# Padding and types of narrow matmuls in two causal attentions: last key block, masks, first query block

## The chip, the cores and the metric

The kernel runs on one core of a Trainium2 chip. The metric is the device time of one launch in microseconds, the median over runs. The core has five engines with instruction streams of their own that wait for each other through semaphores: PE (TensorE, matmuls; its weight loads are listed apart as PEld), DVE (VectorE), ACT (ScalarE), POOL (GpSimd) and SP (here only an issuer of transfers).

## The reference

A hybrid decoder block on 1024 tokens of width 1024, with 16 learned meta tokens in front. Three groups of heads work side by side on the same normalised input: 8 heads of stick-breaking attention (width 64), a Mamba-2 state-space mixer, and 8 heads of MLA (multi-head latent attention). Their outputs go through one output projection, then comes a SwiGLU. What matters here are the two attentions, both causal, in blocks of 128 queries:

```python
# stick-breaking
mask = (kidx[None, :] < qidx[:, None]) & valid[None, :]
z = jnp.einsum('bqhd,bkhd->bhqk', qb, kf) * scale
log_1m = jnp.where(mask, jax.nn.log_sigmoid(-z), 0.0)
between = lax.cumsum(log_1m, axis=3, reverse=True) - log_1m
w = jnp.exp(jnp.where(mask, jax.nn.log_sigmoid(z) + between, -jnp.inf))
out = jnp.einsum('bhqk,bkhd->bqhd', w, vf)
...
# MLA
mask = (kidx[None, :] <= qidx[:, None]) & valid[None, :]
s = jnp.einsum('bqhd,bkhd->bhqk', qb, kf) * scale
p = jax.nn.softmax(jnp.where(mask, s, -1e30), axis=-1)
out = jnp.einsum('bhqk,bkhd->bqhd', p, vf)
```

## The kernel before

**Precision.** Most matmuls take 4-byte operands in the type `F32R` (fp32r, a reduced fp32 that PE takes in one instruction). To keep fp32 accuracy a value is split in two: `hi` is its copy in F32R (by ACT), `lo` is value minus `hi` (by DVE or POOL), and a product becomes three matmuls: hi by hi, lo by hi, hi by lo. The profile writes both F32 and F32R matmul operands as `f32`. Some smaller products, as those of the state-space mixer (lines 797, 801, 810) and the row spreading (line 181), are in plain F32.

**Stages, in the order of time.** The first projections (to about 82 us); stick-breaking attention in four pairs of heads (82 to 482 us), with projections of the next pair and the convolutions of the mixer (`conv_unit`, through `dense_fm`, lines 137 to 139) woven in; the mixer's chunks and the latent projections (to 687 us); MLA, head by head (687 to 1085 us), with the gates of the mixer (`gate_units`) and the first output rows (`out_rows`) woven in; the rest of the output projection and the SwiGLU (to the end).

**Who sets the order.** The program is written stage by stage; a planner with a timeline model puts the instructions of each engine in an order that mixes stages by priority and readiness. On each engine the instructions then run in that order.

**A row of scores.** Keys are counted with the 16 meta tokens first, so query block i (0 to 7) sees 16 + 128 (i + 1) keys. `key_chunks(i)` (line 46) cuts them into chunks of at most 512 columns. For block 0 there are 144 keys, and the chunk is `max(n, 256)` = 256 columns wide: the matmul computes 112 columns that nobody reads. `sb_row` (line 654) makes two F32R matmuls per chunk (lines 662, 663), `mla_row` (line 945) three (960 to 962). In the last chunk of a row the causal mask is added by one more matmul into the same PSUM bank: identity (weights) times a 128x128 mask of 0 and -1e30 (lines 666 and 965), both in bf16 (`identb`, `sb_mask`, `mla_mask`, made at lines 97 to 114). Then ACT or DVE reads the bank, only up to column `n_all - c0`.

**The weighted values.** `weighted_values` (line 293) takes two query blocks at a time, 2j (`pe_even`) and 2j + 1 (`pe_odd`), for j = 0 to 3. PE transposes the weights in groups g = 0 to j of two key blocks each (lines 325, 327), ACT and DVE split them into `ph` and `pl` (`split`, lines 306 to 312), and `accumulate` multiplies them with the values into the bank `out`. A key block has 256 columns: 128 for the odd query block, then 128 for the even one. In the last group (g = j) the second key block is seen by the odd query block only. Its other 128 columns, 384 to 511 of `ph` and `pl`, are set to zero by POOL (lines 330, 331) so that the product is 256 wide all the same, and its two matmuls (lines 300, 301) close the accumulation. There are 8 heads in each attention and 4 values of j, so 64 last groups in all.

**Other names that matter below.** `load_w` (line 119) loads and splits a weight tile through the buffer with the tag `wraw`, of which there is one. `spread` (line 176) and all transposes use `ident`, the 128x128 identity.

Of the kernel before, what the change touches and what calls it, by code (L numbers as in the profile page):

```python
# [11 lines left out]
F32 = mybir.dt.float32  # L12
F32R = mybir.dt.float32r
BF16 = mybir.dt.bfloat16
I32 = mybir.dt.int32
AF = mybir.ActivationFunctionType
ALU = mybir.AluOpType
# [20 lines left out]
NEG = -1e30  # L38
# [7 lines left out]
def key_chunks(i):  # L46
    n = 16 + 128 * (i + 1)
    if n <= 512:
        return [(0, max(n, 256))]
    blocks = i + 1  # L50
    if n <= 1024 and blocks <= 7:
        first = (blocks + 1) // 2 if blocks < 7 else 3
        a = 16 + 128 * first
        return [(0, a), (a, n - a)]
    a = 16 + 128 * 2
    return [(0, a), (a, 384), (a + 384, 384)]
# [3 lines left out]
def tile_hybrid_block(ctx: ExitStack, tc: tile.TileContext, a: dict):  # L60
    nc = tc.nc
    act, dve, pool, pe, sp = nc.scalar, nc.vector, nc.gpsimd, nc.tensor, nc.sync
# [6 lines left out]
    def f32(ap):  # L69
        return ap.bitcast(F32)  # L70
# [3 lines left out]
    const = ctx.enter_context(tc.tile_pool(name="const", bufs=1))  # L74
# [19 lines left out]
    s_inv = dram.tile([MLA_HEADS, SEQ], F32, name="s_inv")  # L94


    ident = const.tile([128, 128], F32, name="ident")
    make_identity(nc, ident)
    identb = const.tile([128, 128], BF16, name="identb")
    act.activation(identb, ident, AF.Identity)  # L100
    ones = const.tile([128, 128], F32, name="ones")
    dve.memset(ones, 1.0)
    zcol = const.tile([128, 1], F32, name="zcol")
    dve.memset(zcol, 0.0)
    halfcol = const.tile([128, 1], F32, name="halfcol")
    dve.memset(halfcol, 0.5)
    sb_mask = const.tile([128, 128], BF16, name="sb_mask")
    mla_mask = const.tile([128, 128], BF16, name="mla_mask")
    for m, base in ((sb_mask, -1), (mla_mask, 0)):
        pool.memset(m, 0.0)  # L110
        pool.affine_select(
            out=m, in_=m, pattern=[[-1, 128]], compare_op=ALU.is_ge, fill=NEG,
            base=base, channel_multiplier=1,
        )
    gmix = const.tile([128, KT], F32, name="gmix")
    sp.dma_start(gmix, a["gmix"])

# [175 lines left out]
    def weighted_values(tp, pvp, work, j, rows, V, hh, dram_out, pm, base=None):  # L293

        pe_even, pe_odd = rows
        out = pvp.tile([128, 512], F32, tag="pv", name="pv")

        def accumulate(blk, ph, pl, c, last):
            if last:
                pe.matmul(out[:64, :256], V[:, blk, hh, 0:64], pl[:, c : c + 256], start=False, stop=False)  # L300
                pe.matmul(out[:, :256], V[:, blk, hh, :], ph[:, c : c + 256], start=False, stop=True)
            else:
                pe.matmul(out[:, :256], V[:, blk, hh, :], ph[:, c : c + 256], start=False, stop=False)  # L303
                pe.matmul(out[:64, :256], V[:, blk, hh, 0:64], pl[:, c : c + 256], start=False, stop=False)

        def split(pt, n):
            nb = 4 if work is not sbb else 2
            ph = work.tile([128, 512], F32R, tag="ph", bufs=nb, name="ph")
            pl = work.tile([128, 512], F32R, tag="pl", bufs=nb, name="pl")
            act.copy(ph[:, :n], pt[:, :n])  # L310
            dve.tensor_tensor(pl[:, :n], pt[:, :n], f32(ph[:, :n]), op=ALU.subtract)  # L311
            return ph, pl

        pt = tp.tile([128, 512], F32, tag="tp", name="ptm")
        pe.transpose(pt[:META, 0:128], pe_odd[:, 0:META], ident)
        pe.transpose(pt[:META, 128:256], pe_even[:, 0:META], ident)
        act.copy(pm[:META], pt[:META, :256])
        dve.tensor_tensor(pm[32 : 32 + META], pt[:META, :256], f32(pm[:META]), op=ALU.subtract)
        pe.matmul(out[:, :256], V[:, 0, hh, :], pm, start=True, stop=False)
        for g in range(j + 1):  # L320
            last = g == j
            pt = tp.tile([128, 512], F32, tag="tp", name="ptg")
            for e in range(2):
                k0 = META + 128 * (2 * g + e)
                pe.transpose(pt[:, e * 256 : e * 256 + 128], pe_odd[:, k0 : k0 + 128], ident)  # L325
                if not (last and e == 1):
                    pe.transpose(pt[:, e * 256 + 128 : e * 256 + 256], pe_even[:, k0 : k0 + 128], ident)  # L327
            ph, pl = split(pt, 384 if last else 512)
            if last:
                pool.memset(f32(ph[:, 384:512]), 0.0)  # L330
                pool.memset(f32(pl[:, 384:512]), 0.0)
            accumulate(2 * g + 1, ph, pl, 0, False)
            accumulate(2 * g + 2, ph, pl, 256, last)
        half = work.tile([64, 256], F32, tag="half", bufs=1, name="half")
        if base is None:
            act.copy(half, out[64:128, :256])
        else:
            for e in range(2):
                c = slice(128 * e, 128 * (e + 1))
                i = 2 * j + 1 - e  # L340
                act.activation(half[:, c], out[64:128, c], AF.Identity, bias=base[64:128, hh, i : i + 1])
        oT = work.tile([64, 256], F32, tag="oT", bufs=2, name="oT")
        dve.tensor_tensor(
            oT.rearrange("p (b t) -> p b t", b=2)[:, ::-1, :],
            out[:64, :256].rearrange("p (b t) -> p b t", b=2),
            half.rearrange("p (b t) -> p b t", b=2),
            op=ALU.add,
        )
        act.dma_start(dram_out[:, 256 * j : 256 * (j + 1)], oT)
# [286 lines left out]
    for i, (q0, qn) in enumerate(((0, 256), (256, 384), (640, 384))):  # L636
# [3 lines left out]
        c0, n = CH_ALL[i]  # L640
# [8 lines left out]
    with ctx_sb as st:  # L649
        sbb = st.enter_context(tc.tile_pool(name="sbb", bufs=2, side="right", reuse_waits="tile"))  # L650
        sc = st.enter_context(tc.tile_pool(name="sc1", bufs=3, space=PSUM, reuse_waits="tile"))
        pvp = st.enter_context(tc.tile_pool(name="pv1", bufs=1, space=PSUM, reuse_waits="tile"))

        def sb_row(Qh, Kh, KSh, i):
            n_all = META + 128 * (i + 1)
            cm = sbb.tile([128, T], F32, tag="cm", bufs=4, name="cm")
            qs = Qh[:, 128 * i : 128 * (i + 1)]
            chunks = key_chunks(i)
            for c0, n in chunks[::-1]:
                ps = sc.tile([128, 512], F32, tag="sc", name="sc_ps")  # L660
                last = c0 + n >= n_all
                pe.matmul(ps[:, :n], qs, Kh[:, c0 : c0 + n], start=True, stop=False)
                pe.matmul(ps[:, :n], qs, KSh[:, c0 : c0 + n], start=False, stop=not last)
                if last:
                    m0 = n_all - 128 - c0
                    pe.matmul(ps[:, m0 : m0 + 128], identb, sb_mask, start=False, stop=True)
                    n = n_all - c0
                act.activation(cm[:, c0 : c0 + n], ps[:, :n], AF.Sigmoid, scale=-0.125)  # L668
            rev = cm[:, 0:n_all][:, ::-1]
            dve.tensor_tensor_scan(rev, rev, zcol.to_broadcast([128, n_all]), 1.0, ALU.mult, ALU.add)  # L670
            return cm

        pms = meta_tiles(sbb)

        def sb_attend(p, proj, values):
            Q, K, KS = proj
            for h in range(2):
                for j in range(NQ // 2):  # L680
                    rows = [sb_row(Q[h], K[h], KS[h], 2 * j + e) for e in range(2)]
                    weighted_values(tp, pvp, sbb, j, rows, values[0], h, s_osb[p, 64 * h : 64 * (h + 1)], pms[j % 2], values[1])

        values = load_value_steps(sbv, sbb, 0)
        step_sizes()
        convs = [8, 9, 10, 11, 0, 1, 2, 3, 4, 5, 6, 7]
        for p in range(4):
            sb_attend(p, proj, values)
            if p < 3:
                if p == 1:  # L690
                    sb_values(1, [load_w(a["w_sbv"][1, u]) for u in range(2)], range(9))
                proj, k_evac, q_evac = sb_project(p + 1)
                dense_fm(dpool, load_w(a["w_sbk"][p + 1]), KT, 128, hn_mov, CH_ALL, k_evac)
                dense_fm(dpool, load_w(a["w_sbq"][p + 1]), KT, 128, hn_real, CH_REAL, q_evac)
                values = load_value_steps(sbv, sbb, p + 1)
            for u in convs[3 * p : 3 * p + 3]:
                conv_unit(u)
# [224 lines left out]
    with ExitStack() as st:  # L922
# [22 lines left out]
        def mla_row(proj, i, total):  # L945
# [11 lines left out]
            for x, (c0, n) in enumerate(chunks):  # L957
# [4 lines left out]
                pe.matmul(ps[:, :n], qh, KL[:96, c0 : c0 + n], start=False, stop=not last)  # L962
                if last:
                    m0 = n_all - 128 - c0
                    pe.matmul(ps[:, m0 : m0 + 128], identb, mla_mask, start=False, stop=True)
                    n = n_all - c0
                dve.tensor_reduce(sm[:, x : x + 1], ps[:, :n], AX.X, ALU.max, negate=True)
                banks.append((ps, c0, n))
# [24 lines left out]
        V = None  # L993
# [760 lines left out]
```

## Time and profile before

| | |
|---|---|
| median of 3 runs | 1889.12 us (1889.0 to 1889.23) |
| the profiled execution | 1887.26 us, of which its span 1885.5 |
| mean granted TensorE clock | 0.962 |

The profile covers one execution. Times are from the start of the span. A row of the page's list of groups, or of the list by line, reads: line, engine, operation, what is written and what is read, the shape of the weights and of the moving operand or output, type, count; then the busy time in us and the mean duration of one in ns; then the idle time of the engine just before these instructions, and what ended it. A row in order of time reads: start, length in us, engine, line, operation, operands, count. Busy time of PE is the union of durations that overlap each other, and their ends are modelled; so distances between starts tell more of what a matmul costs. In a table of stretches the columns are: the stretch, its length, then the busy time and the count for PE, PEld, DVE, ACT and POOL (with a filter only those engines that it leaves), the granted clock, the busy share of the DMA engines and the GB/s.

### The profile page before, as it was taken

Reading aid. Unit: us, or ns where it says so; the run is one execution under the profiler, and the core shown is the slowest. Engines: PE = TensorE matmul, PEld = TensorE weight load, DVE = VectorE, ACT = ScalarE, POOL = GpSimd, SP = SyncE. Lnnn points to the kernel's source line nnn. Section 1 sums busy time; section 2 is a strip of 40 time slices with the busy share of each in tenths; the row PEclk is TensorE's granted clock in tenths of the full one; section 3 lists DMA queues with packets and bytes.
Section 4 is the critical chain, followed back from the end, with each engine's and each line's share of the span. In section 5 each row is a group of like instructions: output and inputs, shape, how many; then the busy total and the mean of one; then the engine's idle time right before and its main releaser. Section 6 shows DMA issues by size and latency. Waiting matters only on the chain.

```text
span 1885.5 us, 26687 instructions
## 1 busy us (share of the span) xinstructions
PE 1730.0 (92%) x9724; PEld 1501.6 (80%) x9724; DVE 1322.4 (70%) x2025; ACT 866.0 (46%) x1881; POOL 880.6 (47%) x707
## 2 busy tenths in 40 slices
PE   8889999999999889996989778889999999799997
PEld 7879989999877679985878657678888888677787
DVE  8888567776546734455565699986667766899956
ACT  7555555555566546674444234432222223433333
POOL 3443244243565465553221266653344333688782
PEclk9999999999999989997999889999999999899998
DMA  4221132122634554454332513122222224733102
GB/s 151 56 73 64 57 80 74 52 60 72 167 105 139 180 164 106 107 130 150 57 72 91 129 50 112 49 86 79 82 88 83 76 75 136 280 100 109 47 0 90
DMA packets 124615, 182.75 MB, mean 97 GB/s; under 512 B 29490, under 2 KB 86804, under 8 KB 124484
## 3 DMA queue, kind: packets, MB, share of 16 engines
q1 hardware_dynamic: 105088, 165.49, 29.3%
q10 hardware_dynamic: 19396, 15.56, 2.7%
q8 instruction: 76, 1.25, 0.3%
q14 instruction: 55, 0.45, 0.1%
HBM read 129.51 MB, written 51.50 MB: 96 GB/s over the span
## 4 chain that ended last, share of the span: by engine, by line
PE 61%; DVE 15%; DMA 7%; issue 4%; POOL 3%; ACT 3%; SPq 1%; ACTq 0%; DVEq 0%; POOLq 0%
PE b_ps L1327 7%; PE b_ps L1329 7%; PE b_ps L1328 7%; PE d_ps L137 6%; PE d_ps L139 6%; PE d_ps L138 6%; DVE raw L1070 2%; DMA gy<-s_y 2%; PE b_ps L1528 2%; PE b_ps L1530 2%; PE b_ps L1529 2%; DVE op L1067 2%; PE ptg L325 1%; DMA raw<-s_ossm 1%; PE pv L303 1%
## 5 line engine op out<-in xcount | busy, mean ns | idle before, releaser
L137 PE MATMUL d_ps<-hnh,whi 128*128 128x384 f32 (+6 forms) x744 | 248.9, 335 | 7.8 <-DVE go L535 4.0
L139 PE MATMUL d_ps<-hnl,whi 128*128 128x384 f32 (+6 forms) x744 | 246.1, 331 | 0.0
L138 PE MATMUL d_ps<-hnh,wlo 128*128 128x384 f32 (+6 forms) x744 | 245.9, 331 | 0.0
L126 POOL TENSOR_TENSOR wlo<-wraw,whi 128x1024 fp32r<-128x1024 f32 (+1 forms) x51 | 124.7, 2445 | 180.9 <-ACT whi L124 171.8
L1067 POOL TENSOR_TENSOR op<-raw,op 128x512 fp32r<-128x512 f32 x113 | 174.3, 1573 | 57.2 <-ACT op L1066 54.0
L137 PEld LDWEIGHTS d_ps<-hnh,whi 128*128 128x128 f32 (+1 forms) x744 | 140.9, 189 | 12.9 <-DVE go L535 5.5
L311 DVE TENSOR_TENSOR pl<-ptg,ph 128x512 fp32r<-128x512 f32 (+1 forms) x160 | 99.5, 629 | 64.5 <-ACT ph L310 62.8
L138 PEld LDWEIGHTS d_ps<-hnh,wlo 128*128 128x128 f32 (+1 forms) x744 | 140.7, 189 | 2.3 <-issue 0.2
L139 PEld LDWEIGHTS d_ps<-hnl,whi 128*128 128x128 f32 (+1 forms) x744 | 140.6, 189 | 2.4 <-issue 0.2
L1327 PE MATMUL b_ps<-T,wh 128*128 128x512 f32 x352 | 138.4, 394 | 0.7 <-ACT T L1066 0.7
L1066 ACT CAST op<-raw 128x512 fp32r<-128x512 f32 x149 | 84.1, 618 | 117.2 <-PE d_ps L1530 46.9
L1328 PE MATMUL b_ps<-T,wl 128*128 128x512 f32 x352 | 137.1, 390 | 0.5 <-POOL wl L1067 0.5
L1329 PE MATMUL b_ps<-T,wh 128*128 128x512 f32 x352 | 137.6, 392 | 0.0
L1067 POOL TENSOR_TENSOR wlo<-raw,whi 128x1024 fp32r<-128x1024 f32 (+1 forms) x22 | 53.0, 2410 | 150.5 <-ACT whi L1066 150.5
L670 DVE TENSOR_TENSOR_SCAN cm<-cm,zcol 128x144 f32<-128x144 f32 (+3 forms) x64 | 101.2, 1586 | 13.0 <-ACT cm L668 12.2
L310 ACT CAST ph<-ptg 128x512 fp32r<-128x512 f32 (+1 forms) x160 | 85.6, 543 | 36.7 <-PE ptg L327 28.7
L1067 POOL TENSOR_TENSOR wl<-raw,wh 128x512 fp32r<-128x512 f32 x46 | 70.6, 1545 | 62.2 <-ACT wh L1066 62.2
L1070 DVE TENSOR_TENSOR raw<-raw 128x512 f32<-128x512 f32 x58 | 70.9, 1227 | 40.4 <-DMA raw<-in_w_gate_dram 35.8
L1066 ACT CAST wh<-raw 128x512 fp32r<-128x512 f32 x88 | 53.0, 616 | 73.7 <-PE b_ps L1329 66.0
L492 POOL TENSOR_TENSOR csig<-csig,cacc 128x384 f32<-128x384 f32 (+1 forms) x36 | 47.8, 1328 | 83.0 <-ACT csig L491 50.6
L487 DVE SCALAR_TENSOR_TENSOR cacc<-d_ps,cw,cacc 128x384 f32<-128x384 f32 (+3 forms) x108 | 61.8, 573 | 33.6 <-ACT cacc L480 31.5
L1528 PE MATMUL b_ps<-op 128*128 128x512 f32 x183 | 73.7, 408 | 12.6 <-DVE hF L1073 11.3
(447 smaller groups left out, 5434.3 us busy)
## 6 DMA issues: line engine op xcount, KB each, us to landing
raw<-in_w_gate_dram SPq DMA_DIRECT2D x22, 512.0 KB
raw<-in_w_up_dram SPq DMA_DIRECT2D x22, 512.0 KB
s_hid<-gs SPq DMA_DIRECT2D x44, 256.0 KB
raw<-in_w_down_dram SPq DMA_DIRECT2D x22, 512.0 KB
raw<-s_hid SPq DMA_DIRECT2D x22, 512.0 KB
wraw<-in_w_xbc_dram SPq DMA_DIRECT2D x12, 512.0 KB
wraw<-in_w_o_dram SPq DMA_DIRECT2D x10, 512.0 KB
s_xs<-csig SPq DMA_DIRECT2D x24, 192.0 KB
```

What stands on the lines that cost most here:

```text
L126: pool.tensor_tensor(lo[:, :cols], raw[:, :cols], f32(hi[:, :cols]), op=ALU.subtract)
L137: pe.matmul(ps[:m, :n], wh, mh, start=(kt == 0), stop=False)
L138: pe.matmul(ps[:m, :n], wl, mh, start=False, stop=False)
L139: pe.matmul(ps[:m, :n], wh, ml, start=False, stop=(kt == nkt - 1))
L670: dve.tensor_tensor_scan(rev, rev, zcol.to_broadcast([128, n_all]), 1.0, ALU.mult, ALU.add)
L1066: act.copy(hi, value)
L1067: eng.tensor_tensor(lo, value, f32(hi), op=ALU.subtract)
L1070: dve.tensor_tensor(out, x, y, op=ALU.subtract)
L1327: pe.matmul(banks[j], hi[:, ks], UH[u][k], start=start and k == 0, stop=False, skip_group_check=skip)
L1328: pe.matmul(banks[j], lo[:, ks], UH[u][k], start=False, stop=False, skip_group_check=skip)
L1329: pe.matmul(banks[j], hi[:, ks], UL[u][k], start=False, stop=stop and k == 3, skip_group_check=skip)
L1528: pe.matmul(banks[o], wh[:, os], hh, start=first, stop=False, skip_group_check=not start)
```

## The change

The last key block of a group is multiplied with its 128 own query columns only, and is taken before the block next to it, so that the full 256 columns are closed last; the memsets go. The masks and the identity that multiplies them become F32R, made in an F32 scratch tile and copied by ACT; `ident` becomes an F32 view of the F32R identity. `key_chunks(0)` is 144 columns wide instead of 256.

```diff
 def key_chunks(i):
     n = 16 + 128 * (i + 1)
     if n <= 512:
-        return [(0, max(n, 256))]
+        return [(0, n)]
...
-    ident = const.tile([128, 128], F32, name="ident")
-    make_identity(nc, ident)
-    identb = const.tile([128, 128], BF16, name="identb")
-    act.activation(identb, ident, AF.Identity)
+    scratch = wa.tile([128, 1024], F32, tag="wraw", bufs=1, name="masks")
+    make_identity(nc, scratch[:, 0:128])
+    identr = const.tile([128, 128], F32R, name="identr")
+    act.copy(identr, scratch[:, 0:128])
+    ident = f32(identr)
...
-    sb_mask = const.tile([128, 128], BF16, name="sb_mask")
-    mla_mask = const.tile([128, 128], BF16, name="mla_mask")
-    for m, base in ((sb_mask, -1), (mla_mask, 0)):
-        pool.memset(m, 0.0)
+    sb_mask = const.tile([128, 128], F32R, name="sb_mask")
+    mla_mask = const.tile([128, 128], F32R, name="mla_mask")
+    for e, (m, base) in enumerate(((sb_mask, -1), (mla_mask, 0))):
+        full = scratch[:, 128 * (e + 1) : 128 * (e + 2)]
+        pool.memset(full, 0.0)
         pool.affine_select(
-            out=m, in_=m, pattern=[[-1, 128]], compare_op=ALU.is_ge, fill=NEG,
+            out=full, in_=full, pattern=[[-1, 128]], compare_op=ALU.is_ge, fill=NEG,
             base=base, channel_multiplier=1,
         )
+        act.copy(m, full)
...
-        def accumulate(blk, ph, pl, c, last):
+        def accumulate(blk, ph, pl, c, n, last):
             if last:
-                pe.matmul(out[:64, :256], V[:, blk, hh, 0:64], pl[:, c : c + 256], start=False, stop=False)
-                pe.matmul(out[:, :256], V[:, blk, hh, :], ph[:, c : c + 256], start=False, stop=True)
+                pe.matmul(out[:64, :n], V[:, blk, hh, 0:64], pl[:, c : c + n], start=False, stop=False)
+                pe.matmul(out[:, :n], V[:, blk, hh, :], ph[:, c : c + n], start=False, stop=True)
...
-            if last:
-                pool.memset(f32(ph[:, 384:512]), 0.0)
-                pool.memset(f32(pl[:, 384:512]), 0.0)
-            accumulate(2 * g + 1, ph, pl, 0, False)
-            accumulate(2 * g + 2, ph, pl, 256, last)
+
+            blocks = [(2 * g + 1, 0, 256), (2 * g + 2, 256, 128 if last else 256)]
+            for blk, c, n in blocks[:: -1 if last else 1]:
+                accumulate(blk, ph, pl, c, n, last and c == 0)
...
-                    pe.matmul(ps[:, m0 : m0 + 128], identb, sb_mask, start=False, stop=True)
+                    pe.matmul(ps[:, m0 : m0 + 128], identr, sb_mask, start=False, stop=True)
...
-                    pe.matmul(ps[:, m0 : m0 + 128], identb, mla_mask, start=False, stop=True)
+                    pe.matmul(ps[:, m0 : m0 + 128], identr, mla_mask, start=False, stop=True)
```

More of the change, by code (lines that the diff above doesn't have):

```diff
@@ L296, in weighted_values @@
         out = pvp.tile([128, 512], F32, tag="pv", name="pv")
-        def accumulate(blk, ph, pl, c, last):
+        def accumulate(blk, ph, pl, c, n, last):
             if last:
-                pe.matmul(out[:64, :256], V[:, blk, hh, 0:64], pl[:, c : c + 256], start=False, stop=False)
-                pe.matmul(out[:, :256], V[:, blk, hh, :], ph[:, c : c + 256], start=False, stop=True)
-            else:
-                pe.matmul(out[:, :256], V[:, blk, hh, :], ph[:, c : c + 256], start=False, stop=False)
-                pe.matmul(out[:64, :256], V[:, blk, hh, 0:64], pl[:, c : c + 256], start=False, stop=False)
+                pe.matmul(out[:64, :n], V[:, blk, hh, 0:64], pl[:, c : c + n], start=False, stop=False)
+                pe.matmul(out[:, :n], V[:, blk, hh, :], ph[:, c : c + n], start=False, stop=True)
+            else:
+                pe.matmul(out[:, :n], V[:, blk, hh, :], ph[:, c : c + n], start=False, stop=False)
+                pe.matmul(out[:64, :n], V[:, blk, hh, 0:64], pl[:, c : c + n], start=False, stop=False)
         def split(pt, n):
```

## The prediction

> **What bounds the kernel now.** I read the page's first two parts for the engines, then the busy time by stage around the two attention passes (the stretches with the edited code), then the instructions in order of time, then the chain of waits.
>
> ```profile
> span 1885.5 us, 26687 instructions
> PE 1730.0 (92%) x9724; PEld 1501.6 (80%) x9724; DVE 1322.4 (70%) x2025; ACT 866.0 (46%) x1881; POOL 880.6 (47%) x707
> PE 61%; DVE 15%; DMA 7%; issue 4%; POOL 3%; ACT 3%; SPq 1%; ACTq 0%; DVEq 0%; POOLq 0%
> ```
>
> ```profile
> 82.00:150.00 68.00, 58.06 (x342) 52.16 (x341) 53.90 (x89) 36.01 (x74) 30.04 (x27) 0.95 0.26 66
> 150.00:482.00 332.00, 329.90 (x2277) 314.55 (x2276) 227.41 (x323) 180.86 (x407) 118.72 (x130) 1.00 0.23 69
> 687.00:850.00 163.00, 152.70 (x1039) 143.46 (x1039) 77.87 (x188) 111.65 (x273) 97.46 (x100) 0.98 0.52 122
> 850.00:900.00 50.00, 36.25 (x190) 31.29 (x189) 28.89 (x63) 19.89 (x48) 15.77 (x17) 0.76 0.50 150
> 900.00:950.00 50.00, 50.00 (x289) 42.94 (x288) 25.89 (x57) 23.09 (x57) 11.16 (x13) 1.00 0.32 66
> 950.00:1000.00 50.00, 43.11 (x225) 35.92 (x225) 33.44 (x55) 21.78 (x48) 15.16 (x13) 0.93 0.23 50
> 1000.00:1053.00 53.00, 51.58 (x291) 43.31 (x290) 35.67 (x72) 20.56 (x54) 8.39 (x11) 1.00 0.35 115
> 1053.00:1085.00 32.00, 21.55 (x103) 17.82 (x103) 16.15 (x26) 9.12 (x19) 8.85 (x7) 0.79 0.57 136
> ```
>
> The columns after the stretch are its length, then busy time of PE, PEld, DVE, ACT and POOL. The first two rows are stick-breaking attention: from 150 us on PE is busy for 329.90 of 332 us, because projections and convolutions fill every gap, so each microsecond added to PE there is a microsecond of span. The other six are MLA: PE is busy 355.2 of 398 us, and some of the rest is waiting for transfers. Everything the change adds or removes in bulk is PE work in these stretches.
>
> What a product costs is the distance between starts, not the duration (durations overlap):
>
> ```profile
> 908.85 0.28 PE L303 MATMUL pv<-ph,V 128*128 128x256 f32 x1
> 908.97 0.28 PE L304 MATMUL pv<-pl,V 128*64 128x256 f32 x1
> 909.08 0.28 PE L300 MATMUL pv<-pl,V 128*64 128x256 f32 x1
> 909.20 0.28 PE L301 MATMUL pv<-ph,V 128*128 128x256 f32 x1
> 909.32 0.40 PE L138 MATMUL d_ps<-raw,wlo 128*128 128x512 f32 x1
> 909.55 0.39 PE L139 MATMUL d_ps<-raw,whi 128*128 128x512 f32 x1
> ```
>
> Four 256-column products in F32R take 909.32 - 908.85 = 0.47 us, 0.118 each; 512 columns take 0.23. A column thus costs (0.23 - 0.118)/256 = 0.44 ns.
>
> **The change part by part.** The costs stand against the profiled execution, 1887.26 us (1885.5 of span and 1.8 around it); the median of the runs is 1889.12, 1.9 more.
>
> *What it touches, counted.* Last key block: two products (L300, L301) in each of 64 groups shrink from 256 to 128 columns, 128 products. Masks: 128 products (64 and 64) keep 128 columns and go from bf16 to F32R. First query block: two scores products in 8 heads and three in 8 more, 40, shrink from 256 to 144 columns.
>
> ```profile
> L304 PE MATMUL pv<-pl,V 128*64 128x256 f32 x256 | 69.6, 292 | 8.0 <-DVE pl L311 8.0
> ...
> L300 PE MATMUL pv<-pl,V 128*64 128x256 f32 x64 | 18.3, 286 | 0.0
> L301 PE MATMUL pv<-ph,V 128*128 128x256 f32 x64 | 18.2, 284 | 0.0
> ...
> L965 PE MATMUL sc_ps<-mla_mask,identb 128*128 128x128 bf16 x64 | 15.3, 239 | 0.0
> L666 PE MATMUL sc_ps<-sb_mask,identb 128*128 128x128 bf16 x64 | 14.7, 230 | 0.0
> ```
>
> So 296 products end up in F32R below 256 columns. All the F32R products I found are 256 to 512 columns wide: the price of a narrow one is not in the trace, and it decides the case. Bounds from the nearest rows:
>
> ```profile
> 564.21 1.11 PE L797 MATMUL yo<-bc,S 128*128 128x128 f32 x8
> 565.15 0.39 PE L765 MATMUL R<-A,sel 80*128 80x128 bf16 x4
> ```
>
> ```profile
> 910.91 0.27 PE L315 MATMUL ptm<-ident,pr 128*16 128x128 f32 x1
> 911.02 0.27 PE L316 MATMUL ptm<-ident,pr 128*16 128x128 f32 x1
> ```
>
> ```profile
> 496.51 0.17 PE d_ps L137
> 496.68 1.05 PE sps L810 x2
> ```
>
> Low end: bf16 at 128 columns, four in 0.39 us, (0.39 - 0.22)/3 = 0.057 us each (0.22 is the duration of one). Middle: a 128-column transpose of 4-byte data, 0.11 from start to start though its weights are only 16 wide. High end: products of 4-byte operands in plain F32. L797 is run 64 times (8 chunks, 2 groups, 4 tiles) and the page counts x128: each product is two instructions. Four products take 1.11 us, (1.11 - 0.28)/7 = 0.119 per instruction, 0.24 per 128-column product. L810 says the same at 512 columns: 1.05 us for its two instructions, against 0.23 in F32R, over four times as much.
>
> I take the fall to the plain rate, because the yo product is the nearest in shape and type (128*128, 128 columns, 4 bytes). Four times 0.44 ns for 128 columns is 0.225; with 0.24 from yo I use **0.23 us**, and for 144 columns 0.26.
>
> [...]
>
> *Last key block.* Each product goes from 0.118 to 0.23: 0.112 x 128 = **+14.3 us** of PE, half in each attention. The new order inside the group (own block first) changes no count; its second product needs `pl` sooner, but PE has other work queued, and the wait for `pl` in L304 was 8.0 us over all 256.
>
> *Masks.* What one costs now:
>
> ```profile
> 904.65 0.34 PE L962 MATMUL sc_ps<-mlo,mhi 96*128 96x384 f32 x1
> 904.83 0.23 PE L965 MATMUL sc_ps<-mla_mask,identb 128*128 128x128 bf16 x1
> 904.87 0.48 PE L138 MATMUL d_ps<-raw,wlo 128*128 128x512 f32 x1
> 905.18 0.39 PE L139 MATMUL d_ps<-raw,whi 128*128 128x512 f32 x1
> ```
>
> From L962 to L139 pass 0.53 us, of which L962 itself is 0.17 (384 columns: 0.118 + 128 x 0.44 ns) and L138 0.23: 0.13 remain for the mask. At 0.23 this is 0.10 x 128 = **+12.8 us**. Below this lies the possibility that the weights load earlier than now:
>
> ```profile
> L965 PEld LDWEIGHTS <-identb 128*128 128x128 bf16 x64 | 6.4, 101 | 7.9 <-issue 6.0
> L303 PEld LDWEIGHTS pv<-ph,V 128*128 128x128 f32 x256 | 49.4, 193 | 12.8 <-ACT ph L310 9.5
> ```
>
> The bf16 identity loads in 0.101 us with 7.9 us of idle ahead of it; a 4-byte one takes 0.193 but starts under the product before it. At best the mask costs 0.06, a gain of 0.07 each; I put that in the first rival.
>
> *First query block.* 0.26 against 0.118: 0.142 x 40 = **+5.7 us**, of which 16 products (2.3) are in the first attention, 24 (3.4) in MLA. Its reduction and activation already read 144 columns and stay.
>
> *The memsets* leave POOL: 64 of `ph`, as below, and as many of `pl`.
>
> ```profile
> L330 POOL MEMSET ph<- 128x128 f32 x64 | 13.1, 205 | 85.9 <-PE pv L303 68.3 <-PE pv L301 16.4 <-issue 1.2
> ```
>
> POOL stands 85.9 us at them, waiting for PE to release `ph`; weight splits queue behind. But no PE wait in either attention is put down to POOL above 1 us and the fullest stretch has PE at 99%, so I value their removal at zero; where PE waits in MLA it could be worth 0 to 3 us.
>
> *The start.* ACT copies three 128x128 tiles instead of one, after POOL's selects.
>
> ```profile
> 1.96 0.30 POOL L111 TENSOR_SCALAR_AFFINE_SELECT mla_mask<-mla_mask 128x128 bf16<-128x128 bf16 x1
> 2.09 0.31 ACT L100 ACTIVATE identb<-ident 128x128 bf16<-128x128 f32 x1
> 4.58 0.52 ACT L242 ACTIVATE hnh<-xT,gmix 128x272 fp32r<-128x272 f32 x1 [2.18 <-DMA xT<-in_xT_dram]
> ```
>
> ACT idles from 2.4 to 4.58 for the first input, so two more copies of 0.31 fit: zero; without that cover 0.6 us. The scratch tile shares its one buffer with `load_w`, first needed long after these copies.
>
> *Sum.* PE work: 14.3 + 12.8 + 5.7 = 32.8 us, that is 7.15 + 6.4 + 2.3 = 15.9 in the first attention and 7.15 + 6.4 + 3.4 = 17.0 in MLA. On the path: in the first attention nearly all, 15.5, since 53 of its 64 masks lie in the 99% stretch:
>
> ```profile
> 150.00:482.00 332.00, 12.16 (x53) 5.07 (x53) 1.00 0.23 69
> ```
>
> In MLA the chain of waits has transfers that added PE work can slide under:
>
> ```profile
> by line: PE d_ps L137 10.6%; PE d_ps L138 10.1%; PE d_ps L139 10.0%; DMA gy<-s_y 9.2%; DMA raw<-s_ossm 6.2%; issue 6.1%; DMA s_inv<-inv 3.0%; PE sc_ps L960 2.7%; DMA raw<-s_osb 2.5%; PE ptg L325 2.5%; PE sc_ps L961 2.4%; PE sc_ps L962 2.4%;
> ```
>
> The shares are of the chain between 687 and 1085 us: 9.2 + 6.2 + 3.0 + 2.5 = 20.9% of it is DMA, which does not grow; with smaller waits I let a quarter of the added work vanish: 0.75 x 17.0 = 12.8. Together +28.3: 1887.26 + 28.3 = 1915.6 for a profiled run, 1917 for the median.
>
> **The rivals.**
>
> *Narrow F32R runs at full column rate (ends faster).* For it: F32R is linear from 512 down to 256 columns and nothing in the trace forbids 128; bf16 does it. Place and price: the two narrow products of a last group at 0.06, saving 2 x 0.058 x 64 = 7.4 us, since the weights loaded behind them are 64 wide; masks bounded by the 128-wide 4-byte load behind them at about 0.12, saving 0.01 x 128 = 1.3; first block bounded by the same, 0. Of 8.7 some 0.86 lie on the path (the shares above): 7.5, giving 1882. If loads do not bind, masks and first block add 0.07 x 128 + 0.05 x 40 = 11, some 1873. It decides as soon as a narrow product is under 0.118.
>
> *A narrow product costs what the padded one did: the change does not save what it says.* For it: the transposes' 0.11 at 128 columns. Then last groups save 0.008 x 128 = 1, masks 0.02 x 128 = 2.5, first block nothing: at most 3, so 1886 to 1889.
>
> *Slow, but MLA hides it.* Then only the first attention pays: 1889 + 15.5 + 3 = 1908. Against it: PE is 94 to 100% busy in 266 of MLA's 398 us.
>
> **How the numbers follow.** Plain rate below 256 columns: 0.64 (0.10 of it the last rival); full rate: 0.22; as before: 0.14. A measurement of this kernel tells about 0.2%, 3.8 us, from no change. Faster 0.21 (the full rate, less a little for work moved by the planner), same 0.14, slower 0.65. The forecast is 1917. Its own range runs from 1906 (the last rival, at nine tenths of the price) to 1926 (all 32.8 us on the path, and 0.24 for 0.23, some 4 more). To leave out no more than 2 in 10 the range has to reach the faster case: 1880 to 1926.
>
> **What would show it.** Right: narrow L300/L301 products 0.22 to 0.24 apart or two instructions each, masks likewise, PE busy some 30 us more, mostly in the two attentions, all other stretches unchanged. Wrong: starts 0.06 apart (first rival) or 0.11 to 0.12 (second). The MLA share is wrong if that stage grows by under 6 or over 17 us; the zero for POOL if stretches without PE idle shrink.

## The result, and the profile after

The changed kernel takes 1880.53 us (median of 19 runs), the kernel before 1886.96 in the same series: ratio 0.9963, with an interval of 0.9953 to 0.9973. It is about 7 us faster; 1917 was forecast. The first rival, a narrow product at full column rate with 1882, is what happened.

From the page of the changed kernel, the span and the engines:

```profile
span 1872.2 us, 26482 instructions
PE 1721.4 (92%) x9724; PEld 1507.1 (80%) x9724; DVE 1312.8 (70%) x2025; ACT 867.2 (46%) x1883; POOL 861.9 (46%) x579
```

The count of PE instructions is the same (x9724), so no product was broken into two, and POOL has 128 fewer. PE is busy 8.6 us less than in the profile before (1721.4 for 1730.0); in the repeats of both kernels (e8 and e9 below) it is 5.2 less. The profiled execution took 1873.88 us, the lowest of the 19, so its distance to the profile of before (13.4 us) is no measure of the change.

A last group of the changed kernel in the order of time (start, length):

```profile
906.01 0.28 PE L307 MATMUL pv<-pl,V 128*64 128x256 f32 x1
906.13 0.22 PE L306 MATMUL pv<-ph,V 128*128 128x128 f32 x1
906.19 0.22 PE L307 MATMUL pv<-pl,V 128*64 128x128 f32 x1
906.25 0.28 PE L303 MATMUL pv<-pl,V 128*64 128x256 f32 x1
906.36 0.28 PE L304 MATMUL pv<-ph,V 128*128 128x256 f32 x1
906.48 0.40 PE L140 MATMUL d_ps<-raw,whi 128*128 128x512 f32 x1
```

The two narrow products start 0.06 us before their successors, the 256-column ones 0.11 to 0.12. The forecast had 0.23. A mask, and the first query block:

```profile
895.93 0.22 PE L967 MATMUL sc_ps<-mla_mask,identr 128*128 128x128 f32 x1
895.99 0.34 PE L962 MATMUL sc_ps<-mhi 96*128 96x272 f32 x1
896.17 0.28 PE L963 MATMUL sc_ps<-mhi,mlo 96*128 96x272 f32 x1
896.29 0.29 PE L964 MATMUL sc_ps<-mlo,mhi 96*128 96x272 f32 x1
```

A 272-column product takes 0.12 (896.17 to 896.29), so of the 0.24 from the mask's start to L963 the mask has 0.12; before it had 0.13. The first query block is from the repeat of the changed kernel (e9 below):

```profile
909.38 0.28 PE L963 MATMUL sc_ps<-mhi,mlo 96*128 96x144 f32 x1
909.50 0.28 PE L964 MATMUL sc_ps<-mlo,mhi 96*128 96x144 f32 x1
909.61 0.27 PE L967 MATMUL sc_ps<-mla_mask,identr 128*128 128x128 f32 x1
```

At 144 columns the products are still 0.11 to 0.12 apart. All three, each read at one place, are the rival's numbers: 7.4 + 1.3 + 0 = 8.7 us of PE.

### The profile page after: what moved, and what is told of

Its sections match the earlier page's. It is cut to its first block, busy times and chain, and to the rows that moved or that the text cites. A ratio compares the mean times of both kernels' runs of the same rounds, so it can differ in the third digit from the quotient of the medians.

```text
span 1872.2 us, 26482 instructions
## 1 busy us (share of the span) xinstructions
PE 1721.4 (92%) x9724; PEld 1507.1 (80%) x9724; DVE 1312.8 (70%) x2025; ACT 867.2 (46%) x1883; POOL 861.9 (46%) x579
## 4 chain that ended last, share of the span: by engine, by line
PE 63%; DVE 15%; DMA 6%; issue 4%; POOL 3%; ACT 3%; SPq 0%; DVEq 0%; ACTq 0%; POOLq 0%
PE d_ps L140 7%; PE b_ps L1329 6%; PE b_ps L1331 6%; PE b_ps L1330 6%; PE d_ps L141 6%; PE d_ps L142 6%; DVE raw L1072 2%; DMA gy<-s_y 2%; PE b_ps L1530 2%; PE b_ps L1532 2%; PE b_ps L1531 2%; DVE op L1069 2%; PE ptg L328 1%; PE ptg L330 1%; PE pv L307 1%
## 5 line engine op out<-in xcount | busy, mean ns | idle before, releaser
L1075 DVE TENSOR_TENSOR hF<-hF,b_ps 128x512 f32<-128x512 f32 (+1 forms) x96 | 59.0, 634 | 35.7 <-PE b_ps L1596 18.5
```

## The experiments

Three theories were put against each other: COLUMNS (the price of a narrow product), POOL (the memsets that are gone), ORDER (the planner lays the stages out otherwise). The kernel before runs at 1887 us on the chip of the first result and at 1874 to 1878 on those of the experiments, so only ratios to the kernel before, timed on the same chip, are compared.

**The price by itself (e5).** Series of 24 products of one shape on one input tile:

```diff
+    def series(src, weights, n, count=24):
+        for i in range(count):
+            w = src[:, 512 + 8 * i : 512 + 8 * i + weights]
+            nc.tensor.matmul(ps[:weights, :n], w, src[:, 0:n], start=(i == 0), stop=(i == count - 1))
```

> Not the block but series of 24 matmuls of one form each, on x alone: F32R with weights 128, 64 and 16 wide and 512 to 64 columns, then bf16 and plain F32. Theory COLUMNS: distance between starts is the larger of 0.44 ns per column and the load of the next weights (0.84 ns per weight column, 0.11 us for 128), plus some ns: with 128-wide weights 0.23 at 512, then flat at 0.11 to 0.12 from 256 down to 64; with 64-wide weights 0.12 at 256, 0.06 at 128 and 64; plain F32 two instructions per product. The forecast's theory (plain rate below 256): 0.22 at 128 columns whatever the weights.

Stretches from inside a series (start, length of all, how many); `128*64` is weights 64 wide, `p<-r` F32R, `p<-b` bf16, `p<-x` plain F32:

```profile
27.01 2.40 PE L32 MATMUL p<-r 128*128 128x256 f32 x19
35.13 2.40 PE L32 MATMUL p<-r 128*128 128x128 f32 x20
37.77 2.40 PE L32 MATMUL p<-r 128*128 128x64 f32 x20
50.20 2.38 PE L32 MATMUL p<-r 128*64 128x256 f32 x19
56.65 1.31 PE L32 MATMUL p<-r 128*64 128x128 f32 x19
75.74 1.36 PE L32 MATMUL p<-r 128*16 128x128 f32 x20
91.49 1.22 PE L32 MATMUL p<-b 128*128 128x128 bf16 x19
129.50 4.96 PE L32 MATMUL p<-x 128*128 128x128 f32 x43
```

Less the duration of the last one (0.22 to 0.28), divided by the count less one: with 128-wide weights 0.118 at 256 columns and 0.112 at both 128 and 64; with 64-wide weights 0.117 at 256 and 0.060 at 128; with 16-wide weights 0.060 at 128. So an F32R product costs the larger of its columns and a load of weights, and there is no step at 256. That it is the load of the next weights, and not of its own, the last group above shows: L306 has 128-wide weights and takes 0.06 (906.13 to 906.19) in front of 64-wide ones. bf16 with 128-wide weights is 0.056 at 128 columns, so it is not held up in this way. Plain F32 with 128-wide weights takes 0.112 per instruction, twice per product, 0.22: the forecast's price was right for such a series in plain F32, and narrow F32R isn't that. The Trainium skill, "TensorE: Matmul & The Clock Gate", section "LDWEIGHTS (loading the stationary operand)", gives the time of a load as its columns divided by 1.2, in ns; an estimate from it for 128 columns is 107 ns. The flat 0.112 agrees with it, for 4-byte weights.

**One part at a time (e1, e2, e3).** The kernel before, with one of the three edits of the diff each:

```diff
 e1   the last key block: accumulate() with n, own block first, no memsets
 e2   the masks: scratch, identr, sb_mask and mla_mask in F32R
 e3   key_chunks: return [(0, n)]
```

> The kernel before with the change to the last key block alone (narrow products, own block first, no memsets); masks stay bf16, the first query block 256 wide. Theory COLUMNS (a narrow F32R product runs at the full column rate, bounded only by the load of the weights behind it): starts 0.06 us apart, 7.4 us of PE less, 5 to 7 us of time: ratio 0.9965. Theory POOL (the gain comes from the memsets that are gone): the same ratio here, but lost again where the memsets are kept. Theory ORDER (the gain is the planner's other order of the stages, not the price of a product): any ratio between 0.995 and 1.005, not the sum of the parts.

> The kernel before with the masks and their identity in F32R alone. Theory COLUMNS: a mask costs 0.12 us for 0.13 because the 128-wide weights behind it take 0.11 to load: 1.3 us of PE less, ratio 0.9993 and no difference that can be told. Theory ORDER: up to 0.5% either way.

> The kernel before with 144 columns for the first query block alone. Theory COLUMNS: 40 products stay bounded by the 128-wide weights behind them, 0.12 us as at 256 columns: ratio 1.000. Were the columns alone to count, 0.05 x 40 = 2 us less, 0.999. Theory ORDER: up to 0.5% either way.

Measured: e1 0.992 (0.9906 to 0.9933), e2 0.999 (0.9977 to 1.0002), e3 0.9968 (0.9957 to 0.998). The masks came out as COLUMNS has them. The other two did not: e1 gains twice its 7.4 us, and e3 gains 6 us with no product that became cheaper. The parts sum to -1.2%, the whole is -0.4%. Something that no part's price contains is worth as much as the change.

**The memsets (e4).**

```diff
             ph, pl = split(pt, 384 if last else 512)
+            if last:
+                pool.memset(f32(ph[:, 384:512]), 0.0)
+                pool.memset(f32(pl[:, 384:512]), 0.0)
```

> The changed kernel with the two memsets of each last group kept; the columns that they write are not read any more. Theory COLUMNS: the gain stays, ratio to the kernel before 0.9965. Theory POOL: the gain goes, 1.000, and POOL stands some 80 us at the memsets again.

0.9964 (0.9951 to 0.9977), the ratio of the changed kernel, though POOL stands at them as before (list by line; the column after the bar is its idle time ahead of them):

```profile
L333 POOL MEMSET ph<- 128x128 f32 x64 | 13.0, 203 | 83.7 <-PE pv L306 69.5 <-PE pv L304 14.1
```

POOL falls: 84 us of waiting there cost nothing that can be told.

**Repeats and neighbours (e8 to e11).** Both kernels again, and each with another width for the first query block, which changes no price by more than 0.01 us:

```diff
 e10, on the kernel before
-        return [(0, max(n, 256))]
+        return [(0, max(n, 272))]
 e11, on the changed kernel
-        return [(0, n)]
+        return [(0, max(n, 256))]
```

> The kernel before, unchanged, on the same chip as the next three, with a profile: ratio 1.000 within 0.2%. Its MLA stage should again hold the wait of PE for the row `grow` (10.6 us in the first profile).

> The changed kernel, unchanged, on the same chip. Theory COLUMNS: 8.7 us of PE less than the kernel before, 0.9955. It should still hold the wait for `grow`, as in its first profile. Theory ORDER: the ratio is 0.996 like that of the part with 144 columns alone, so nothing of it can be put down to the narrow products.

> The kernel before with 272 columns for the first query block, for 256: 40 products of 0.125 us for 0.118, 0.3 us more PE work, so a change of work that can't be told. Theory COLUMNS alone: ratio 1.000. Theory ORDER (the planner's other order moves the time by as much as the parts do): 0.995 to 1.005, with another wait in the MLA stage.

> The changed kernel with 256 columns for the first query block as before; narrow last key block and F32R masks stay. PE work as in the changed kernel, since 144 columns are bounded by the load of the weights. Theory COLUMNS alone: ratio as the changed kernel, 0.996. Theory ORDER: it can be that of the last key block alone, 0.992, if the wait for `grow` is gone.

Measured: e8 0.9997 (0.9986 to 1.0007), e9 0.9959 (0.9945 to 0.9973), e10 1.0005 (0.9992 to 1.0017), e11 0.9919 (0.9905 to 0.9933). So the changed kernel *loses* 0.4% by 144 columns, where the kernel before gained 0.3% by them (e3). The waits of PE from 685 to 1100 us differ; the largest ones of e9 (changed kernel) and of e11 (the same with 256 columns): what waited for what, us in total, times, longest:

```profile
PE b_ps L1183 <- ACT op L1068: 8.8, 1, 8.8
PE d_ps L140 <- ACT grow L708: 8.1, 1, 8.1
PE pv L306 <- ACT ph L313: 5.5, 1, 5.5
```

```profile
PE b_ps L1183 <- DVE oT L345: 5.3, 1, 5.3
PE d_ps L184 <- DVE dg L183: 4.6, 1, 4.6
PE d_ps L140 <- ACT raw L1025: 4.2, 1, 4.2
```

In e9 PE waits 8.1 us for `grow`, the row that scales the mixer's output; in e11 not. ACT in the order of time, e9 and then e11:

```profile
868.90 1.04 ACT L1025 CAST raw<-raw 128x1024 fp32r<-128x1024 f32 x1 [8.80 <-DMA raw<-s_osb]
869.85 0.59 ACT L708 ACTIVATE grow<-d_ps 128x512 f32<-128x512 f32 x1
870.34 0.59 ACT L977 ACTIVATE pr<-sc_ps,sm 128x400 f32<-128x400 f32 x1
```

```profile
863.56 0.60 ACT L708 ACTIVATE grow<-d_ps 128x512 f32<-128x512 f32 x1
864.48 0.59 ACT L977 ACTIVATE pr<-sc_ps,sm 128x400 f32<-128x400 f32 x1 [0.32 <-PE ptg L330]
...
873.12 1.04 ACT L1025 CAST raw<-raw 128x1024 fp32r<-128x1024 f32 x1 [6.66 <-DMA raw<-s_osb]
```

The brackets give the idle time before the instruction, and what ended it. In e9 the copy of an output row of the first attention (L1025), whose transfer is not there yet, stands ahead of `grow` and of MLA's exponentials; ACT waits 8.80 us, and PE with it. In e11 the planner put the copy behind them, and PE works on for a while; then it waits 4.2 us for the copied row itself (`raw`, L1025, above). So this place accounts for about 4 us of the 8 between e9 (1871.15 us) and e11 (1862.93). The edits don't touch these lines: they only shift what the planner has ready at that moment. MLA, from its first split to its last output, and the rest of the span, e9 and then e11 (length, then PE and the others):

```profile
687.10:1064.40 377.30, 347.50 (x2137) 315.48 (x2135) 213.34 (x457) 205.98 (x497) 149.88 (x98) 0.96 0.44 111
1064.40:1868.40 804.00, 737.82 (x3244) 600.77 (x3243) 628.76 (x791) 276.38 (x473) 435.24 (x274) 0.96 0.28 93
690.40:1057.90 367.50, 339.52 (x2099) 307.79 (x2099) 210.51 (x452) 205.50 (x497) 146.53 (x98) 0.96 0.46 114
1057.90:1861.20 803.30, 744.02 (x3273) 603.95 (x3273) 629.95 (x796) 275.23 (x473) 429.42 (x275) 0.96 0.27 93
```

MLA is 9.8 us shorter in e11, but PE idles only 1.8 us less there (28.0 for 29.8); it is busy 8.0 us less, with 38 products fewer. Behind MLA stand 29 products more, and they cost no length: PE idles 6.9 us less there (59.3 for 66.2). So the wait for `grow` marks the two orders; it doesn't by itself make up the difference between them.

The kernels fall into two groups by this wait of 8 to 11 us. With it: the kernel before 1, e10 1.0005, e2 0.999, the changed kernel 0.9963 and 0.9959, e4 0.9964. Without it: e3 0.9968, e1 0.992, e11 0.9919. Inside each group the edits with the narrow last block are worth nearly the same: 0.0036 to 0.0041 (7 to 8 us) in the first, 0.9968 to 0.992, 0.0048 (9 us), in the second. With intervals of 0.001 to 0.0014 either way of each ratio, that agrees with 7.4 us.

**Taking the copy off ACT (e12).** The changed kernel with

```diff
                 if src is s_osb:
-                    act.copy(hi, raw)
+                    pool.tensor_copy(hi, raw)
```

> The changed kernel (144 columns kept) with the copies of the four stick-breaking output rows (line 1025) on POOL for ACT, so that no copy that waits for a transfer stands ahead of `grow` and of MLA's exponentials on ACT. If that place on ACT is what takes the changed kernel from 0.992 back to 0.996, the wait of PE for `grow` is gone and the ratio is 0.990 to 0.993. If it stays at 0.996, the wait is only moved, or 144 columns cost by themselves.

0.9934 (0.9916 to 0.9952), just above the range that was expected. No wait for `grow` is among the waits of PE in that stretch, but 10.5 us, in 7 pieces, for `hT` (L1043). By its middle value the kernel with 144 columns is some 0.3% faster without the copy on ACT. So the place of the copy is likely a part of what 144 columns cost; as the interval meets that of e9, this is not shown.

**The forecast's price, put in by hand (e6).** The 296 narrow products of the changed kernel in plain F32 (the same edit at the last block and at the first query block):

```diff
-                    pe.matmul(ps[:, m0 : m0 + 128], identr, sb_mask, start=False, stop=True)
+                    pe.matmul(ps[:, m0 : m0 + 128], ident, f32(sb_mask), start=False, stop=True)
```

> The changed kernel with its 296 narrow products issued in plain F32, that is at the price which the forecast took for them. If the forecast's step from PE work to time was right (0.86 of it on the path), this costs about 33 us of PE over the 256-wide ones and lands near 1917, ratio 1.015; if MLA hides its half, 1908, ratio 1.010; if all of it shows, 1.018.

1.0225 (1.021 to 1.024), 42 us over the kernel before. At 0.22 per product the added PE work would be about 30 us (0.105 x 128 + 0.09 x 128 + 0.13 x 40). The page of e6 has more: PE is busy for 1781.8 us, 52 us longer than the 1730.0 before. A part of the surplus stands in the last groups:

```profile
312.57 0.43 PE L307 MATMUL pv<-pl,V 128*64 128x128 f32 x2
312.94 0.33 PE L303 MATMUL pv<-pl,V 128*64 128x256 f32 x1
313.11 0.28 PE L304 MATMUL pv<-ph,V 128*128 128x256 f32 x1
313.23 0.27 PE L331 MATMUL ptg<-identr,cm 128*128 128x128 f32 x1
```

From the plain L307 to the start behind the group pass 0.66 us; in the changed kernel, where L307 is F32R, 0.29 (906.19 to 906.48). That is 0.37 more, and the price has 0.16 (0.22 for 0.06). The 0.2 us that are left make up some 13 us in 64 groups like this one. So a plain product in front of these F32R ones costs more than in a series of its own; why, no run shows. Of the 52 us of PE work 42 showed in the time, 0.81.

**A further step (e7, e13).** If the 64 masks of stick-breaking cost 0.12 us each in a stretch that PE fills, a select on POOL after the sigmoid is cheaper:

```diff
-                pe.matmul(ps[:, :n], qs, KSh[:, c0 : c0 + n], start=False, stop=not last)
-                if last:
-                    m0 = n_all - 128 - c0
-                    pe.matmul(ps[:, m0 : m0 + 128], identr, sb_mask, start=False, stop=True)
-                    n = n_all - c0
+                pe.matmul(ps[:, :n], qs, KSh[:, c0 : c0 + n], start=False, stop=True)
                 act.activation(cm[:, c0 : c0 + n], ps[:, :n], AF.Sigmoid, scale=-0.125)
+                if last:
+                    own = cm[:, n_all - 128 : n_all]
+                    pool.affine_select(out=own, in_=own, pattern=[[-1, 128]], compare_op=ALU.is_ge,
+                                       fill=1.0, base=-1, channel_multiplier=1)
```

e13 is e7 with 256 columns for the first query block.

> The changed kernel with the 64 mask products of stick-breaking replaced by a select on POOL, which sets the masked weights to 1 after the sigmoid (sigmoid of +infinity). Theory COLUMNS: 64 products of 0.12 us leave a stretch where PE is 99% busy, 6 to 7.7 us less than the changed kernel, ratio to the kernel before about 0.993. Rival: the scan on DVE now waits for POOL, where splits of 2.4 us run in front: no gain over the changed kernel, 0.9965, or a loss if PE runs dry.

> The stick-breaking mask on POOL, as in the run before with it, and 256 columns for the first query block. If that run was 0.983 through 7.7 us of mask products less and an order without the wait for `grow`, this one has the same products, and its ratio is 0.992 - 0.004 = 0.988 or lower with an order that is good, above 0.990 with one that has the wait.

e7: 0.9831 (0.9813 to 0.985), 1842.08 us where the kernel before takes 1874.03: the best version found, and faster than the 0.993 that was expected. e13: 0.9966 (0.9954 to 0.9977), and its PE waits 7.9 us for `grow` again:

```profile
PE d_ps L140 <- ACT grow L710: 7.9, 1, 7.9
```

Against their neighbours in the same group, e13 gains nothing on the changed kernel (0.9963) and e7 0.9% on e11 (0.9919), 17 us. Their mean, some 8 us, is near the 7.7 that were expected, but neither run is, so what the masks cost in time is not shown. The wait for `grow` and the slow products after it may explain part of the 25 us between e7 and e13; the rest is open.

## Why the prediction was wrong

- **The price of a narrow F32R product: wrong, and it decided the case.** The step that failed is "I take the fall to the plain rate, because the yo product is the nearest in shape and type". Shape and 4 bytes were alike, the form of the instruction was not: the yo product is two instructions, an F32R product one at any width. Measured 0.060 where 0.23 was taken (e5 and the changed kernel's own rows). That no row had F32R below 256 columns said nothing of its price, and the straight line from 512 to 256 columns pointed on to 0.06. The "over four times" of L810 sets a length, 1.05, against a distance between starts; by distances e5 has 0.86 for a plain product of 512 columns, 3.7 times the 0.23.
- **Last key block:** +14.3 forecast, -7.4 by starts, the rival's figure; shown by the narrow starts, and the time in both groups of kernels agrees.
- **Masks:** +12.8 forecast, -1.3 by starts; e2 alone can't be told from no change.
- **First query block:** +5.7 forecast, 0 by starts, for the 128-wide weights behind each product take 0.11 to load. In time it moved the kernel by 0.3 to 0.4%, down in one kernel and up in the other, with the order.
- **The memsets at zero, in spite of 85.9 us of POOL waiting:** right (e4).
- **The start at zero:** right. In the changed kernel's profile the three copies of ACT end at 2.8 us, and ACT then waits for the first input until 4.26 us, as before until 4.58.
- **0.86 of the PE work on the path:** e6 fits, with 42 us of time for 52 us of PE work. The price of a plain product was too low in this place, not the share; how much of the 42 us the order made stays open.
- **The rival's 1882 by 8.7 x 0.86:** right in size, 0.9963 being 7 us, but in part by luck: with 256 columns for the first query block, which the rival prices at nothing, the gain is 15 us (e11). "Work moved by the planner" stood in the forecast as a little. It is 0.4% in the changed kernel and up to 1.3% between e7 and e13. That 1880.53 lies just inside the stated range says nothing for the forecast's own mechanism, whose range began at 1906.
- **Where the gain shows:** said to be half in each attention. The repeats on one chip, cut at MLA's first split and its last output: the three stages of e8, then the first stage of e9, whose other two stand above:

```profile
0.00:685.60 685.60, 642.25 (x4348) 589.20 (x4349) 472.23 (x778) 384.14 (x911) 290.61 (x274) 0.98 0.31 97
685.60:1074.70 389.10, 352.98 (x2125) 313.62 (x2125) 218.32 (x456) 206.31 (x497) 158.56 (x160) 0.94 0.44 111
1074.70:1873.80 799.10, 735.03 (x3254) 599.02 (x3253) 624.27 (x792) 275.66 (x473) 436.49 (x274) 0.96 0.27 92
```

```profile
0.00:687.10 687.10, 639.73 (x4346) 595.08 (x4347) 471.52 (x778) 385.62 (x913) 277.16 (x208) 0.97 0.32 97
```

Up to MLA the changed kernel has PE busy 2.5 us less and idle 4.0 us more (47.4 for 43.4), so nothing is gained there. MLA is 11.8 us shorter (377.30 for 389.10), and behind it, where the change touches no product, 4.9 us are lost again (804.00 for 799.10). This is one execution of each. Work that PE is spared in a woven stage need not shorten that stage.

## What to carry to other kernels

Before a cost is taken from the nearest row, look whether that row is the same instruction form: a count that is twice the calls in the code marks another one. An F32R product pays for the larger of its own columns and the weights loaded behind it, so trimming below 256 columns pays only where weights narrower than 128 follow; put the narrow products there. A price from a series of one form need not hold where two forms alternate (e6). Where a planner lays out the order, a change that alters no work can move the time by as much as the change under study. So build neighbours that differ in little but the order, compare kernels that share their largest waits, and follow a wait that is gone through the stages behind it, for it may come back there.

## What was not expected of the hardware

A wait of PE for a transfer costs more than its length. PE around the wait for `grow` in the repeat of the kernel before (length, PE busy and count, then PEld, DVE, ACT, POOL; the last three columns are the granted clock, the DMA share and GB/s):

```profile
860.00:865.00 5.00, 0.36 (x4) 0.17 (x2) 0.29 (x1) 0.00 (x0) 0.00 (x0) 0.95 0.76 95
865.00:870.00 5.00, 1.42 (x3) 1.16 (x4) 0.42 (x1) 3.01 (x8) 1.89 (x1) 0.50 1.01 394
870.00:875.00 5.00, 5.00 (x16) 4.20 (x15) 0.70 (x3) 0.63 (x3) 0.77 (x3) 0.53 1.03 411
875.00:880.00 5.00, 5.00 (x31) 4.38 (x30) 4.70 (x10) 4.37 (x10) 2.52 (x5) 1.00 0.60 230
```

After the idle stretch the granted clock is 0.50 and 0.53 until 875 us, and 512-column products start 0.43 us apart there instead of 0.23:

```profile
869.60 0.63 PE L139 MATMUL d_ps<-raw,whi 128*128 128x512 f32 x1
870.03 0.63 PE L137 MATMUL d_ps<-raw,whi 128*128 128x512 f32 x1
```

The Trainium skill, "TensorE: Matmul & The Clock Gate", section "HAM oscillation — how this bites in real kernels", describes this return to half clock after a few idle microseconds; the rows agree, with 8.2 us idle and then 0.50. In e11 the wait of 4.2 us brings it too, so the half clock is no difference between e9 and e11:

```profile
870.00:875.00 5.00, 0.80 (x3) 0.68 (x3) 0.51 (x2) 1.85 (x4) 0.76 (x1) 0.74 1.00 374
875.00:880.00 5.00, 4.90 (x21) 4.14 (x20) 4.73 (x11) 3.66 (x11) 3.51 (x4) 0.50 1.03 414
```
